# A squared-ReLU MLP: seven block products in place of eight in part of the second product, and a first product in 256 columns

## The chip, the cores and the metric

One core of one Trainium2 chip. The metric is the device time of one execution in microseconds (us), the median of several runs. The engines are named as in the profile: PE is the matrix engine (PEld its loads of the stationary operand), DVE the vector engine, ACT the scalar engine, POOL the general one, SP the queue that issues most DMAs. PSUM is the matrix engine's accumulator memory of eight banks, 512 float32 columns each.

## What is computed

One layer of a decoder: a gated mix of a convolution branch and an attention branch, cross attention, then the MLP, which is where the change lies. SEQ is 256, D_MODEL 1024, D_FF 4096.

```python
        hf = _rmsnorm(h, norm_ffn_g[l]) @ w_ff1[l]
        h = h + jnp.square(jax.nn.relu(hf)) @ w_ff2[l]
    return _rmsnorm(h, norm_final_g)
```

The first product is (256 x 1024)(1024 x 4096), the second (256 x 4096)(4096 x 1024).

## The kernel before

**Split operands.** Every large product is made in float32r with operands split in two: `high` is the operand rounded to float32r (an ACT copy, L189), `low` the rest (a DVE subtraction, issued through `Counted.call`, L77, the line under which all of PE's and DVE's counted work shows). `mm3` (L276) makes one product of three matmuls: high x high, high x low, low x high.

**The weight stream.** All weights come in 1 MB pieces in the order of `STREAM`. `load` (L161) issues the DMA of the next piece on SP into one of three raw buffers, and queues the splitting of its two halves in `high_jobs`; a high queues its low in `low_jobs`; the second low of a piece calls `load` again, so that the next DMA waits until DVE has freed a raw buffer. `weights(kind, i, half, kt)` (L216) hands out a split half; `split_ahead` (L242), called once behind each `weights`, issues one low and one high of later halves. High and low buffers are six each (`HALVES`), counted by `nsplit` and `nused`. If a half is not yet split when it is asked for, `weights` issues splits until it is.

**Order.** Each engine works through its instructions in the order in which the program issues them; the program is one hand-written order. `tick` (L246) steps the generators in `chains`, one `yield` each, so that the work of a later step is issued some matmuls later.

**The first MLP product.** A chunk is 256 of the 4096 hidden columns, as two tiles of 128 (`ct`), each over eight parts of 128 rows of the model dimension (`kt`). Tiles of kind `f1` are "wide" (`is_wide`, L299): per `kt` one matmul of 512 columns (weight high against activation high and low side by side) and one of 256 (weight low against activation high), into both halves of a bank. `activation` (L1082) brings the halves together: ACT evicts one half, DVE adds the other, DVE makes relu(t) times t, ACT makes the high part, DVE the low part.

**The second MLP product.** `ff2` (L1108): for a chunk c, two parts k of 128 hidden columns, two row blocks `rb` of 128 rows and two column halves `hf` of 512, so eight `mm3` of 512 columns a chunk. All 16 chunks accumulate in four banks `dst[rb][hf]`. The loop at L1148 runs the first product two chunks ahead of the second. Behind it the last two chunks (14, 15) are done block by block (`last_products`, L1165), and while PE makes the next block, DVE adds a finished one to the residual (`last_residual`), ACT squares it, and `last_norm` scales and stores a row block.

Of the kernel before, what the change touches and what calls it, by code (L numbers as in the profile page):

```python
# [8 lines left out]
F32 = mybir.dt.float32  # L9
# [3 lines left out]
ALU = mybir.AluOpType  # L13
# [43 lines left out]
HALVES = 6  # L57
EARLY = (3,)
WHOLE = (("conv", 0),)


class Counted:
# [49 lines left out]
def block_kernel(ctx, tc, x, xt, mem, memt, wst, wki, vecs, convw, gout, out):  # L112
# [15 lines left out]
    def t8(name, dt=F32, shape=(P, KT, S)):  # L128
        return big.tile(list(shape), dt, tag="t8", bufs=12, name=name)
# [4 lines left out]
    def w2(name, dt=F32, shape=(P, 512)):  # L134
        return work.tile(list(shape), dt, tag="w2", bufs=8, name=name)
# [25 lines left out]
    def load(parts=1):  # L161
        if nload[0] >= len(STREAM):
            return
        c = nload[0]
        nload[0] += 1
        key = STREAM[c]
        raw = t8(f"raw{c}", F32, (P, N_CHUNK)) if c in EARLY else raws.tile([P, N_CHUNK], F32, tag="raw", name=f"raw{c}")
        n = KT * NK if key[0] == "ki" else N_CHUNK
        src = wki if key[0] == "ki" else wst[INDEX[key]]
        for q in range(parts):  # L170
            ns = slice(q * n // parts, (q + 1) * n // parts)
            nc.sync.dma_start(raw[:, ns], src[:, ns])
        if key in WHOLE:
            whole[key] = raw.rearrange("p (k n) -> p k n", k=2 * KT)
            return
        parts = 1 if key[0] == "ki" else 2
        for q in range(parts):
            ns = slice(q * n // parts, (q + 1) * n // parts)
            high_jobs.append(lambda ns=ns, q=q, last=q == parts - 1: high(key, c, raw, ns, q, last))

    def low_by_dma(key, c, q):

# [2 lines left out]
    def high(key, c, raw, ns, q, last):  # L185
        n = ns.stop - ns.start
        hi = highs.tile([P, N_CHUNK // 2], F32R, tag="hi", name=f"hi{c}_{q}")[:, :n]
        lo = lows.tile([P, N_CHUNK // 2], F32R, tag="lo", name=f"lo{c}_{q}")[:, :n]
        act(hi, raw[:, ns], AF.Copy)  # L189
# [12 lines left out]

        low_jobs.append(low)

    def split_high():
        if high_jobs and nsplit[0] - nused[0] < HALVES - held[0]:
            nsplit[0] += 1
            high_jobs.pop(0)()

    def split_low():  # L210
        if low_jobs:
            low_jobs.pop(0)()

    nsplit, nused, held = [0], [0], [1]

    def weights(kind, i, half, kt):  # L216

        key = (kind, i, half)
        while key not in prepared:
            split_high()  # L220
            split_low()
        nused[0] += 1
        return [w.rearrange("p (k n) -> p k n", k=kt) for w in prepared.pop(key)]


    chains, fill, turn, done = [], [], [0], []
# [852 lines left out]

    start(ff_scale())  # L1080

    def activation(ps, ct, sh, sl):  # L1082
        t = w2(f"ft{ct}", F32, (P, S))
        act(t, ps[:, S:], AF.Copy)  # L1084
        yield
        dve.tensor_tensor(out=t, in0=ps[:, :S], in1=t, op=ALU.add)
        dve.scalar_tensor_tensor(out=t, in0=t, scalar=0.0, in1=t, op0=ALU.max, op1=ALU.mult)
        act(sh, t, AF.Copy)
        yield
        dve.tensor_tensor(out=sl, in0=t, in1=sh.bitcast(F32), op=ALU.subtract)  # L1090

    def ff1(c):
        parts = t8(f"fs{c}", F32R, (P, 4, S))
        jobs = []

        def after(ct, ps):
            jobs.append(start(activation(ps, ct, parts[:, ct % 2, :], parts[:, 2 + ct % 2, :])))

        if c == 0:
            form_b_late("f1", c, f2, after, ps_of=ps_acc)  # L1100
        else:
            form_b("f1", c, f2, after, ps_acc if c == 1 else ps_mm)
        return parts[:, :2, :], parts[:, 2:, :], jobs

    pending = [ff1(0), ff1(1)]
    dst = [[ps_acc(f"ps_ff{rb}{hf}") for hf in range(2)] for rb in range(2)]

    def ff2(c, k, w, x2, rb, hf, cs=slice(0, 512), ps=None, start=False, stop=False):  # L1108
        rows, cols = slice(rb * P, rb * P + P), slice(hf * 512 + cs.start, hf * 512 + cs.stop)
        mm3(dst[rb][hf][:, cs] if ps is None else ps, x2[0][:, k, rows], x2[1][:, k, rows], w[0][:, 0, cols],  # L1110
            w[1][:, 0, cols], start or c == 0 and k == 0, stop)

    hg = turned.rearrange("p (r d) -> p r d", r=2)
    ss = small.tile([P, 2, 3], F32, tag="sso", name="ss_o")
# [5 lines left out]
    def last_residual(rb, ps, lo, hi):  # L1120
        h = h_rm[:, lo // P : hi // P, rb, :]
        ps = by_tiles(ps)
        dve.scalar_tensor_tensor(out=h, in0=ps, scalar=r2[0][:, rb : rb + 1], in1=h, op0=ALU.mult, op1=ALU.add)
# [22 lines left out]
            (nc.scalar if n == 2 else nc.sync).dma_start(out[rb, :, lo:hi], cols)  # L1146

    for c in range(14):  # L1148
        pending.append(ff1(c + 2))
        *x2, jobs = pending.pop(0)  # L1150
        for job in jobs:
            finish(job)
        for k in range(2):
            w = weights("f2", c, k, 1)
            split_ahead()
            for rb in range(2):
                for hf in range(2):
                    ff2(c, k, w, x2, rb, hf)
            tick()
    for *_, jobs in pending:  # L1160
        for job in jobs:
            finish(job)
    ws = {(c, k): weights("f2", c, k, 1) for c in (14, 15) for k in range(2)}

    def last_products(rb, hf, **where):  # L1165
        for (c, k), w in ws.items():
            ff2(c, k, w, pending[c - 14], rb, hf, stop=c == 15 and k == 1, **where)
# [8 lines left out]
    last_products(1, 0)  # L1176
    last_residual(1, dst[1][0], 0, 512)
    last_squares(1, 0, 0, 512)
    last_products(1, 1, cs=slice(0, 256))
    ps = ps_mm("ps_last")[:, :S]  # L1180
    for (c, k), w in ws.items():
        ff2(c, k, w, pending[c - 14], 1, 1, slice(256, 512), ps, c == 14 and k == 0, c == 15 and k == 1)
    last_residual(1, dst[1][1], 512, D)
    last_squares(1, 1, 512, 768)
    last_residual(1, ps, 768, D)
    last_squares(1, 2, 768, D)
    last_norm(1, 2)

# [68 lines left out]
```

## Time and profile before

| what | value |
|---|---|
| median of 3 runs | 508.76 us (508.66 to 508.78) |
| the profiled execution | 508.65 us, span 506.8 us |
| granted PE clock, mean | 0.997 |
| DMA | 100.32 MB, mean 198 GB/s |
| MLP, by the matmuls into `ps_f`, `ps_ff` and `ps_last` | from 322.7 to 500.0 us of the span |

A line of a group reads: line, engine, operation, what it writes and what it reads, shape, count, then busy time in us and mean ns of one, then the engine's idle time just before and who ended most of it. A line of a timeline reads: start in us, duration in us, engine, line, operation, count. Matmuls overlap, and their ends are modelled, so that the distance of their starts is the cost of one in a row. A line of a stretch reads: the stretch, its length, busy time of the engine and its instructions (those that reach in are counted), granted clock, DMA share, GB/s.

### The profile page before, as it was taken

How to read it: one execution, taken by the hardware profiler on the slowest of the kernel's cores; microseconds unless marked ns; L12 is line 12 of the kernel's file. 1: busy time of each engine (PE TensorE's matmuls, PEld its weight loads, DVE VectorE, ACT ScalarE, POOL GpSimd, SP SyncE). 2: the span in 40 equal slices, each digit the busy share in tenths (PEclk: the TensorE clock that was granted, in tenths of full speed). 3: DMA queues.
4: the chain of work that ended last, by engine and by line, in shares of the span. 5: the costliest groups of instructions: out<-in, count | busy, mean ns of one | idle time of the engine just before them, and what ended most of it. 6: DMA issues, size and time to landing. Idle time of an engine off the chain costs nothing.

```text
span 506.8 us, 7855 instructions
## 1 busy us (share of the span) xinstructions
PE 496.5 (98%) x2951; PEld 438.6 (87%) x2951; DVE 419.7 (83%) x806; ACT 314.6 (62%) x565; POOL 31.7 (6%) x49
## 2 busy tenths in 40 slices
PE   7999999999999999999999999999999999999994
PEld 5999998888888888888898999988888888888884
DVE  5999999999999799999899986699755666665565
ACT  7657777878666667678657666575444545544442
POOL 2002212221111100000000000000000000000000
PEclk9999999999999999999999999999999999999998
DMA  8959768899788634437644553445777744455302
GB/s 320 375 185 276 208 182 248 222 262 248 223 279 221 188 113 168 133 116 250 249 164 169 192 214 105 149 157 224 212 242 212 247 167 166 174 211 211 153 1 83
DMA packets 26502, 100.32 MB, mean 198 GB/s; under 512 B 10576, under 2 KB 11472, under 8 KB 15968
## 3 DMA queue, kind: packets, MB, share of 16 engines
q1 hardware_dynamic: 22400, 92.90, 52.5%
q0 software_dynamic: 3632, 6.59, 7.4%
q8 instruction: 23, 0.38, 0.3%
q10 hardware_dynamic: 432, 0.33, 0.2%
q14 instruction: 15, 0.12, 0.1%
HBM read 91.16 MB, written 1.05 MB: 182 GB/s over the span
## 4 chain that ended last, share of the span: by engine, by line
PE 95%; issue 1%; ACT 1%; DMA 1%; DVE 1%; POOLq 0%; POOL 0%; SPq 0%; DVEq 0%; ACTq 0%
PE ps_f L77 18%; PE ps_ff L77 16%; PE ps_conv L77 9%; PE ps_co L77 4%; PE ps_mix L77 4%; PE ps_ao L77 4%; PE ps_q L77 4%; PE ps_k L77 4%; PE ps_ga L77 4%; PE ps_gc L77 4%; PE ps_v L77 4%; PE ps_xo L77 3%; PE ps_qi L77 2%; PE ps_xk L77 2%; PE ps_xv L77 2%; PE ps_xq L77 2%
## 5 line engine op out<-in xcount | busy, mean ns | idle before, releaser
L77 DVE TENSOR_TENSOR lo<-raw,hi 128x1024 fp32r<-128x1024 f32 x163 | 196.8, 1216 | 5.0 <-ACT hi L189 3.4
L189 ACT ACTIVATE hi<-raw 128x1024 fp32r<-128x1024 f32 x163 | 168.8, 1048 | 1.6 <-DMA raw<-in_wst_dram 1.6
L77 PE MATMUL ps_f<-ff_p,hi 128*128 128x512 f32 x256 | 89.5, 396 | 0.0
L77 PE MATMUL ps_ff<-hi,fs 128*128 128x512 f32 (+1 forms) x256 | 80.4, 386 | 0.0
L77 DVE SCALAR_TENSOR_TENSOR acc<-u,cw,acc 128x234 f32<-128x234 f32 (+29 forms) x190 | 78.1, 462 | 0.3
L77 PE MATMUL ps_f<-ff_p,lo 128*128 128x256 f32 x256 | 66.1, 279 | 0.0
L77 PEld LDWEIGHTS ps_ff<-hi,fs 128*128 128x128 f32 x256 | 47.9, 188 | 9.2
L1084 ACT ACTIVATE ft<-ps_f 128x256 f32<-128x256 f32 x32 | 12.3, 383 | 70.0 <-PE ps_f L77 70.0
L77 PEld LDWEIGHTS ps_f<-ff_p,hi 128*128 128x128 f32 x256 | 46.7, 188 | 9.2
L77 DVE TENSOR_TENSOR ft<-ps_f,ft 128x256 f32<-128x256 f32 x32 | 13.5, 422 | 46.0 <-ACT ft L1084 46.0
L77 PEld LDWEIGHTS ps_f<-ff_p,lo 128*128 128x128 f32 x256 | 48.2, 188 | 2.7
L77 PE MATMUL ps_ff<-lo,fs 128*128 128x512 f32 (+1 forms) x128 | 49.4, 386 | 0.0
L77 PE MATMUL ps_conv<-n_p,hi 128*128 128x256 f32 x224 | 41.0, 285 | 0.0
L77 PEld LDWEIGHTS ps_conv<-n_p,hi 128*128 128x128 f32 x224 | 34.9, 192 | 0.8 <-issue 0.7
L77 PE MATMUL ps_conv<-n_p,lo 128*128 128x256 f32 x112 | 31.7, 283 | 0.0
L516 POOL DMA_DIRECT2D acc<-products x25 | 21.6, 866 | 125.3 <-ACT products L515 48.7
L77 PEld LDWEIGHTS ps_ff<-lo,fs 128*128 128x128 f32 x128 | 24.1, 188 | 4.9
L77 PE MATMUL ps_q<-n_p,hi 128*128 128x512 f32 x64 | 23.6, 406 | 0.0
L77 PE MATMUL ps_k<-n_p,hi 128*128 128x512 f32 x64 | 23.5, 407 | 0.0
L77 PE MATMUL ps_ao<-o_p,hi 128*128 128x512 f32 x64 | 22.6, 401 | 0.0
L77 PE MATMUL ps_co<-u_p,hi 128*128 128x512 f32 (+1 forms) x80 | 22.2, 351 | 0.0
L77 PE MATMUL ps_mix<-mix_p,hi 128*128 128x512 f32 (+1 forms) x80 | 22.2, 351 | 0.0
(246 smaller groups left out, 1009.4 us busy)
## 6 DMA issues: line engine op xcount, KB each, us to landing
raw<-in_wst_dram SPq DMA_DIRECT2D x80, 1024.0 KB, 4.9
acc<-products POOLq DMA_DIRECT2D x25, 256.0 KB, 5.0
raw<-in_wst_dram SPq DMA_DIRECT2D x4, 512.0 KB, 7.2
x_rm<-in_x_dram SPq DMA_DIRECT2D x2, 512.0 KB, 4.1
mem_rm<-in_mem_dram SPq DMA_DIRECT2D x1, 1024.0 KB, 8.7
mem_t<-in_memt_dram SPq DMA_DIRECT2D x1, 1024.0 KB, 10.7
h_t<-in_xt_dram SPq DMA_DIRECT2D x1, 1024.0 KB, 7.1
h_rm<-turned SPq DMA_DIRECT2D x16, 64.0 KB, 5.9
```

Of the source, the lines that this page charges most:

```text
L77: return fn(*args, **kwargs)
L189: act(hi, raw[:, ns], AF.Copy)
L516: nc.gpsimd.dma_start(acc[:, ts, :], prod, accum_op=ALU.add)
L1084: act(t, ps[:, S:], AF.Copy)
```

## The change

The chunks fall in three groups: 2, 3, 5, 6, 8, 9, 11 and 12 (`SEVEN`) have their second product made of seven block products; 0, 1, 4, 7 and 10 are made of eight as before, into other banks; 13, 14 and 15 (from `JOINED` on) are done block by block at the end.

- The first product is narrow: per `kt` three matmuls of 256 columns, and both tiles of a chunk share one bank. ACT makes Relu out of PSUM and then Square; nothing is added on DVE.
- For a chunk of seven, four sums of weight blocks are made on DVE (`outer`: two in one operation, `inner`: two, one after the other), four differences of hidden blocks in three DVE operations (`n`), and all of these are split in high and low too. The weights come in four stages: left (2 blocks), last (1), outer (2), inner (2); inner has buffers of its own and takes no slot of the six.
- The halves of `f1` of chunk c + 2 and `f2` of chunk c are split and used alternately: first tile of f1, first half of f2, second tile of f1, second half of f2.
- The seven sums accumulate over all these chunks in seven banks. `combine` adds them to the residual on DVE after the last first-product chunk, and the last three chunks follow.

```diff
+SEVEN = (2, 3, 5, 6, 8, 9, 11, 12)
+JOINED = 13
...
+        if key[0] == "f2" and key[1] < JOINED:
+
+            at = [j.key for j in high_jobs].index(("f1", key[1] + 2, 1))
+            first = len(jobs) // 2
+            high_jobs[at:at] = jobs[:first]
+            jobs = jobs[first:]
+        high_jobs.extend(jobs)
...
+    def seven(key, c, raw):
+
+        b = raw.rearrange("p (k h n) -> p k h n", k=2, h=2)
+        flat = raw.rearrange("p (j n) -> p j n", j=4)
+        t = t8(f"sums{c}", F32, (P, 4, 512))
+        late = t8(f"late{c}", F32R, (P, 2, 2, 512))
+
+        def outer():
+            dve.tensor_tensor(out=t[:, 0:2, :], in0=flat[:, 0:4:3, :], in1=flat[:, 1:2, :].to_broadcast([P, 2, 512]),
+                              op=ALU.add)
+
+        def inner():
+            dve.tensor_tensor(out=t[:, 2, :], in0=t[:, 1, :], in1=flat[:, 0, :], op=ALU.add)
+            dve.tensor_tensor(out=t[:, 3, :], in0=t[:, 2, :], in1=flat[:, 2, :], op=ALU.add)
+
+        def stage(name, src, n, before=None, slot=True):
+            def high():
...
+                act(hi, src, AF.Copy)
+
+                def low():
+                    dve.tensor_tensor(out=lo, in0=src, in1=hi.bitcast(F32), op=ALU.subtract)
+                    prepared[(*key, name)] = (hi, lo)
+                    if name == "inner":
+                        load()
...
+        return [stage("left", b[:, :, 0, :], 2), stage("last", flat[:, 3:4, :], 1),
+                stage("outer", t[:, 0:2, :], 2, outer), stage("inner", t[:, 2:4, :], 2, inner, False)]
...
     def split_low():
         if low_jobs:
             low_jobs.pop(0)()
+        if len(high_jobs) > 1:
+            high_jobs[1].prepare()
...
-        return kind in ("f1", "gc", "ga", "ao", "xk", "q", "k") or (kind in ("mix", "co") and ct < 6)
+        return kind in ("gc", "ga", "ao", "xk", "q", "k") or (kind in ("mix", "co") and ct < 6)
...
+    def activation(c, ct, ps, t, sh, sl):
+        act(t[:, ct, :], ps, AF.Relu)
+        act(t[:, ct, :], t[:, ct, :], AF.Square)
+        yield
...
+        if ct and c < JOINED:
+            n = w2(f"fn{c}", F32, (P, 4, P))
+            if c in SEVEN:
+                dve.tensor_tensor(out=n[:, 0:2, :], in0=flat[:, 1:2, :].to_broadcast([P, 2, P]), in1=flat[:, 0:4:3, :],
+                                  op=ALU.subtract)
+                dve.tensor_tensor(out=n[:, 2, :], in0=flat[:, 0, :], in1=n[:, 1, :], op=ALU.subtract)
+                dve.tensor_tensor(out=n[:, 3, :], in0=flat[:, 2, :], in1=n[:, 2, :], op=ALU.subtract)
...
+        for js, src in cs:
+            act(sh[:, js, :], src, AF.Copy)
+        yield
+        for js, src in cs:
+            dve.tensor_tensor(out=sl[:, js, :], in0=src, in1=sh[:, js, :].bitcast(F32), op=ALU.subtract)
...
+        for name, terms in ((("left", (("1", 0), ("2", 1))), ("last", (("3", 6),))) if half == 0 else
+                            (("outer", (("5", 4), ("7", 3))), ("inner", (("6", 5), ("4", 2))))):
+            w = weights("f2", c, name, None)
+            split_ahead()
+            for j, (bank_name, part) in enumerate(terms):
+                product(bank_name, x.of(part), w, j)
...
     for c in range(14):
+        hidden.append(Hidden(c + 2))
+        ps = ps_mm(f"ps_f{c + 2}")
+        for side in range(2):
+            w = weights("f1", c + 2, side, KT)
             split_ahead()
+            col = ps[:, side * S : side * S + S]
+            tile_b(col, w, f2)
+            hidden[c + 2].after(side, col)
             tick()
+            if c < JOINED:
+                if side == 0:
+                    hidden[c].done()
+                half_of(hidden[c], side)
+                tick()
+    ws = {(c, k): weights("f2", c, k, 1) for c in range(JOINED, 16) for k in range(2)}
...
+    def combine():
+        r, b = r2[0], banks
+        minus = small.tile([P, 2], F32, tag="minus", name="minus")
+        dve.tensor_scalar(minus, r, -1.0, None, ALU.mult)
+        add_to(0, 0, b["2"], r)
+        add_to(0, 1, b["3"], r)
+        add_to(1, 0, b["4"], r)
+        add_to(0, 0, b["1"], r)
+        v, e, g = (w2(f"comb{j}") for j in range(3))
+        act(v, b["1"], AF.Copy)
+        dve.tensor_tensor(out=v, in0=b["6"], in1=v, op=ALU.subtract)
+        dve.tensor_tensor(out=e, in0=b["5"], in1=v, op=ALU.add)
+        add_to(0, 1, e, r)
+        dve.tensor_tensor(out=v, in0=b["7"], in1=v, op=ALU.add)
+        add_to(1, 0, v, minus)
+        dve.tensor_tensor(out=g, in0=b["7"], in1=e, op=ALU.add)
+        add_to(1, 1, g, r)
+
+    for x in hidden[JOINED:]:
+        x.done()
+    combine()
...
+    lasts = [ps_mm("ps_last"), *(banks[name] for name in "2345")]
     for hf in range(2):
-        last_products(0, hf)
-        last_residual(0, dst[0][hf], 512 * hf, 512 * hf + 512)
+        last_products(0, hf, lasts[hf])
+        last_residual(0, lasts[hf], 512 * hf, 512 * hf + 512)
         last_squares(0, hf, 512 * hf, 512 * hf + 512)
     last_norm(0, 1)
```

`add_to` is one DVE operation that scales a block by the row factor and adds it to the residual rows `h_rm`, as `last_residual` does.

More of the change, by code (lines that the diff above doesn't have):

```diff
@@ L175, in load @@
             return
[L176 to L179, printed above, removed]
+        if key[0] == "f2" and key[1] in SEVEN:
+            jobs = seven(key, c, raw)
+        else:
+            parts = 1 if key[0] == "ki" else 2
+            jobs = []
+            for q in range(parts):
+                ns = slice(q * n // parts, (q + 1) * n // parts)
+                jobs.append(Stage((*key, q), lambda ns=ns, q=q, last=q == parts - 1: high(key, c, raw, ns, q, last)))
@@ new lines, in load, with __init__, prepare @@
+        if key[0] == "f2" and key[1] < JOINED:
[4 more added lines that the diff above has]
+        high_jobs.extend(jobs)
+    class Stage:
+        def __init__(self, key, high, before=None, slot=True):
+            self.key, self.high, self.before, self.slot = key, high, before, slot
+        def prepare(self):
+            if self.before:
+                self.before()
+                self.before = None
@@ new lines, in seven @@
+    def seven(key, c, raw):
[11 more added lines that the diff above has]
+            def high():
+                if slot:
+                    hi, lo = ([pool.tile([P, N_CHUNK // 2], F32R, tag=tag, name=f"{tag}{c}{name}")[:, : n * 512]
+                               .rearrange("p (j n) -> p j n", j=n)] for pool, tag in ((highs, "hi"), (lows, "lo")))
+                    hi, lo = hi[0], lo[0]
+                else:
+                    hi, lo = late[:, 0], late[:, 1]
+                act(hi, src, AF.Copy)
[4 more added lines that the diff above has]
+                        load()
+                low_jobs.append(low)
+            return Stage((*key, name), high, before, slot)
+        return [stage("left", b[:, :, 0, :], 2), stage("last", flat[:, 3:4, :], 1),
+                stage("outer", t[:, 0:2, :], 2, outer), stage("inner", t[:, 2:4, :], 2, inner, False)]
@@ L205, in split_high @@
     def split_high():
-        if high_jobs and nsplit[0] - nused[0] < HALVES - held[0]:
-            nsplit[0] += 1
-            high_jobs.pop(0)()
+        if high_jobs and (not high_jobs[0].slot or nsplit[0] - nused[0] < HALVES - held[0]):
+            job = high_jobs.pop(0)
+            nsplit[0] += job.slot
+            job.prepare()
+            job.high()
     def split_low():
@@ L221, in weights @@
             split_low()
-        nused[0] += 1
-        return [w.rearrange("p (k n) -> p k n", k=kt) for w in prepared.pop(key)]
+        nused[0] += half != "inner"
+        return [w if kt is None else w.rearrange("p (k n) -> p k n", k=kt) for w in prepared.pop(key)]
     chains, fill, turn, done = [], [], [0], []
@@ L1092, in ff1 @@
[L1092 to L1111, printed above, removed]
+        flat = t.rearrange("p k (r n) -> p (k r) n", r=2)
+        if c not in SEVEN:
+            cs = [(slice(2 * ct, 2 * ct + 2), flat[:, 2 * ct : 2 * ct + 2, :])]
+        else:
+            cs = [(slice(1, 3), flat[:, 2:4, :]) if ct else (slice(0, 1), flat[:, 0:1, :])]
@@ new lines, in activation @@
+        if ct and c < JOINED:
[5 more added lines that the diff above has]
+                dve.tensor_tensor(out=n[:, 3, :], in0=flat[:, 2, :], in1=n[:, 2, :], op=ALU.subtract)
+                cs.append((slice(3, 7), n))
+            else:
+                dve.tensor_tensor(out=n[:, 0:2, :], in0=flat[:, 0:4:2, :], in1=flat[:, 1:4:2, :], op=ALU.subtract)
+                cs.append((slice(4, 6), n[:, 0:2, :]))
@@ new lines, in activation, with __init__, after, of @@
+        for js, src in cs:
+            act(sh[:, js, :], src, AF.Copy)
+        yield
+        for js, src in cs:
+            dve.tensor_tensor(out=sl[:, js, :], in0=src, in1=sh[:, js, :].bitcast(F32), op=ALU.subtract)
+    class Hidden:
+        def __init__(self, c):
+            self.c, self.jobs = c, []
+            parts = t8(f"fs{c}", F32R, (P, 2, 7, P))
+            self.hi, self.lo = parts[:, 0], parts[:, 1]
+            self.t = w2(f"ft{c}", F32, (P, 2, S))
+        def after(self, ct, ps):
+            self.jobs.append(start(activation(self.c, ct % 2, ps, self.t, self.hi, self.lo)))
+        def of(self, j):
+            return self.hi[:, j, :], self.lo[:, j, :]
+        def row(self, k, rb):
+            return self.of(2 * k + rb)
+        def done(self):
+            for job in self.jobs:
+                finish(job)
@@ new lines, in block_kernel, with product @@
+    hidden = [Hidden(0), Hidden(1)]
+    form_b_late("f1", 0, f2, hidden[0].after, ps_of=ps_acc)
+    form_b("f1", 1, f2, hidden[1].after, ps_acc)
+    uses = {}
+    for c in range(JOINED):
+        for name in ("2", "2", "3", "4", "4", "3", "5", "5") if c not in SEVEN else "1236457":
+            uses[name] = uses.get(name, 0) + 1
+    banks, used = {}, {}
+    def product(name, a, w, j, cs=slice(0, 512)):
+        if name not in banks:
+            banks[name] = {"2": ps_acc, "3": ps_acc, "4": ps_acc, "5": ps_acc, "7": ps_mm}.get(name, ps_aux)(f"ps_p{name}")
+        used[name] = used.get(name, 0) + 1
+        mm3(banks[name], *a, w[0][:, j, cs], w[1][:, j, cs], used[name] == 1, used[name] == uses[name])
@@ new lines, in half_of @@
+    def half_of(x, half):
+        c = x.c
+        if c not in SEVEN:
+            w = weights("f2", c, half, 1)
+            split_ahead()
+            left, right = slice(0, 512), slice(512, D)
+            product("2", x.row(half, 0), w, 0, left)
+            product("4", x.row(half, 1), w, 0, left)
+            product("3", x.of(4 + half), w, 0, right)
+            product("5", x.row(half, 1), w, 0, right)
+            return
+        for name, terms in ((("left", (("1", 0), ("2", 1))), ("last", (("3", 6),))) if half == 0 else
+                            (("outer", (("5", 4), ("7", 3))), ("inner", (("6", 5), ("4", 2))))):
+            w = weights("f2", c, name, None)
+            split_ahead()
+            for j, (bank_name, part) in enumerate(terms):
+                product(bank_name, x.of(part), w, j)
@@ L1159, in block_kernel @@
             tick()
[L1160 to L1165, printed above, removed]
-        for (c, k), w in ws.items():
-            ff2(c, k, w, pending[c - 14], rb, hf, stop=c == 15 and k == 1, **where)
+            if c < JOINED:
[3 more added lines that the diff above has]
+                tick()
@@ new lines, in block_kernel, with last_products, add_to @@
+    ws = {(c, k): weights("f2", c, k, 1) for c in range(JOINED, 16) for k in range(2)}
+    def last_products(rb, hf, ps, cs=slice(0, 512)):
+        cols = slice(hf * 512 + cs.start, hf * 512 + cs.stop)
+        for (c, k), w in ws.items():
+            mm3(ps, *hidden[c].row(k, rb), w[0][:, 0, cols], w[1][:, 0, cols], c == JOINED and k == 0,
+                c == 15 and k == 1)
+    def add_to(rb, hf, ps, scales):
+        h = h_rm[:, 4 * hf : 4 * hf + 4, rb, :]
+        dve.scalar_tensor_tensor(out=h, in0=by_tiles(ps), scalar=scales[:, rb : rb + 1], in1=h, op0=ALU.mult, op1=ALU.add)
@@ L1177, in block_kernel @@
-    last_residual(1, dst[1][0], 0, 512)
+    last_products(1, 0, lasts[2])
+    last_residual(1, lasts[2], 0, 512)
     last_squares(1, 0, 0, 512)
[L1179 to L1183, printed above, removed]
+    last_products(1, 1, lasts[3][:, :S], slice(0, 256))
+    last_products(1, 1, lasts[4][:, :S], slice(256, 512))
@@ L1184, in block_kernel @@
+    last_residual(1, lasts[3][:, :S], 512, 768)
     last_squares(1, 1, 512, 768)
-    last_residual(1, ps, 768, D)
+    last_residual(1, lasts[4][:, :S], 768, D)
     last_squares(1, 2, 768, D)
```

17 lines of the change are left out of this document (removed).

## The prediction

> **What bounds the kernel now.** I read the page's first part, then the chain, then who waited for whom on TensorE.
>
> ```profile
> PE 496.5 (98%) x2951; PEld 438.6 (87%) x2951; DVE 419.7 (83%) x806; ACT 314.6 (62%) x565; POOL 31.7 (6%) x49
> ...
> PE 95%; issue 1%; ACT 1%; DMA 1%; DVE 1%; POOLq 0%; POOL 0%; SPq 0%; DVEq 0%; ACTq 0%
> ...
> PE ps_warm L384 <- DVE zero_r L369: 1.9, 1, 1.9
> PE ps_rsb_n L77 <- POOL rs_n L389: 0.9, 1, 0.9
> PE ps_conv L77 <- DVE n_f L77: 0.6, 1, 0.6
> ```
>
> TensorE is the chain, and the three waits listed are all it ever waited, none of them in the MLP. So a matmul removed there pays in full, but every wait that the change brings is new time. Next, what one MLP chunk costs: stretches of the trace cut at the first matmul of each product, one narrow stage (qi, three tiles), and neighbouring matmuls (start, duration).
>
> ```profile
> core 0: us, PE busy (x), PEclk, DMA share, GB/s
> 33.10:41.74 8.64, 8.64 (x75) 1.00 0.69 238
> 378.51:384.10 5.59, 5.59 (x34) 1.00 1.06 358
> 384.10:389.54 5.44, 5.44 (x26) 1.00 0.27 63
> 477.81:483.39 5.58, 5.58 (x33) 1.00 0.27 112
> ...
> 382.13 0.39 PE L77 MATMUL ps_f<-ff_p,hi 128*128 128x512 f32 x1
> 382.36 0.27 PE L77 MATMUL ps_f<-ff_p,lo 128*128 128x256 f32 x1
> 382.48 0.40 PE L77 MATMUL ps_f<-ff_p,hi 128*128 128x512 f32 x1
> ...
> 62.12 0.28 PE L77 MATMUL ps_conv<-n_p,lo 128*128 128x256 f32 x1
> 62.24 0.40 PE L77 MATMUL ps_conv<-n_p,hi 128*128 128x256 f32 x2
> 62.48 0.28 PE L77 MATMUL ps_conv<-n_p,lo 128*128 128x256 f32 x1
> ```
>
> Durations overlap; starts give the cost. The first product takes 5.59 us a chunk (16 steps of 0.349, one 512 and one 256 wide). The second takes 5.44 (24 matmuls of 0.227). A narrow step, three matmuls of 256, takes 0.360 both in the conv rows and in qi (8.64/24). The granted clock is 1.00 throughout.
>
> **The change, part by part.** The sum is made against the profiled execution: 508.65 us (span 506.8 and 1.85 around it), 0.11 below the median of 508.76.
>
> (1) Eight chunks do 21 matmuls of 512 columns instead of 24: 8 x 3 x 0.227 = **-5.45 us**.
>
> (2) The first product's 256 steps become narrow: 256 x (0.360 - 0.3494) = **+2.7 us**. It has the same columns and one more matmul a step. On the Trainium skill's page "TensorE: Matmul & The Clock Gate", section "Back-to-back issue gap", a matmul costs N/2.4 + 2.5 ns; an estimate by that page is +2.5 ns a step, 0.65 us instead of 2.7. The rows show 10.6 ns, and the rows decide.
>
> (3) DVE and ACT during the MLP. Prices:
>
> ```profile
> L77 DVE TENSOR_TENSOR lo<-raw,hi 128x1024 fp32r<-128x1024 f32 x61 | 73.4, 1221 | 1.8 <-ACT hi L189 0.4
> L189 ACT ACTIVATE hi<-raw 128x1024 fp32r<-128x1024 f32 x61 | 62.5, 1050 | 0.0
> L77 DVE TENSOR_TENSOR ft<-ps_f,ft 128x256 f32<-128x256 f32 x32 | 13.5, 422 | 46.0 <-ACT ft L1084 46.0
> L1088 ACT ACTIVATE fs<-ft 128x256 fp32r<-128x256 f32 x32 | 13.4, 419 | 7.6 <-DVE ft L77 7.5
> L1084 ACT ACTIVATE ft<-ps_f 128x256 f32<-128x256 f32 x32 | 12.3, 383 | 70.0 <-PE ps_f L77 70.0
> L77 DVE TENSOR_TENSOR h_t<-ps_xo,h_t 128x512 f32<-128x512 f32 x3 | 2.1, 692 | 0.7 <-PE ps_xo L77 0.7
> L77 DVE SCALAR_TENSOR_TENSOR h_rm<-ps_ff,ms_ff,h_rm 128x512 f32<-128x512 f32 x4 | 3.0, 748 | 4.2 <-PE ps_ff L77 4.2
> 486.44 2.35 DVE L77 TENSOR_TENSOR lo<-raw,hi 128x1024 fp32r<-128x1024 f32 x2
> ```
>
> Two 1024-wide DVE operations in a row take 2.35, so one behind another costs 1.13; likewise 0.60 for 512, 0.33 for 256 and, off the same slope, 0.20 for 128 (0.29 when it must wait for the one before; bounds 0.16 to 0.42). A seven-product chunk then has on DVE: low parts 5 x 1.13 + 0.60 = 6.25, sums of weights 1.13 + 0.60 + 0.70 = 2.4, differences of the hidden columns (`n`) about 1.0, their low parts 1.1: 10.8 us. TensorE's chunk is 16 x 0.360 + 21 x 0.227 = 10.5. A plain chunk needs about 6 of 11.2. ACT needs near 9 of 10.5 (Relu and Square priced as the 256-wide copies, 0.38 and 0.42). So neither is too slow over three chunks; what counts is the order. What feeds them:
>
> ```profile
> raw<-in_wst_dram SPq DMA_DIRECT2D x27, 1024.0 KB, 4.9
> SPq L172 <- DVE lo L77: 241.3, 47, 10.9
> L189 ACT ACTIVATE hi<-raw 128x1024 fp32r<-128x1024 f32 x163 | 168.8, 1048 | 1.6 <-DMA raw<-in_wst_dram 1.6
> ```
>
> Loads wait for a raw buffer that DVE's last low part frees (241 us of SP waiting), yet ACT waited only 1.6 us for a load: now a freed buffer is next needed two chunks of stream later, some 11 us. The change interleaves halves, so that `f1`'s second low part of one chunk frees the buffer into which the *next* `f2` goes, whose "left" half is split before the next chunk's own `f1` second half. That makes a loop from one such low part to the next: landing 4.9; high of left 1.05; low of left 1.13; `n` 1.0 (issued ahead of what follows, in order); low of last 0.60; outer sum 1.13; low parts of the hidden columns 0.93; low of `f1` 1.22; hand-overs 0.15 = **12.1 us**. Into a plain chunk the parts between fall away: 4.9 + 1.05 + 1.13 + 1.0 + 1.22 + 0.15 = 9.45. From chunk 2 to chunk 12 the loop runs 7 times into a seven-product chunk and 3 times into a plain one: 113 us. TensorE's own way is 7 x 10.5 + 3 x 11.2 = 107.2. Cover at the start: after plain chunk 1 that low part is ready 2.1 us early (Relu and Square 0.9 after the tile, then `n`, last, outer sum, low parts 4.9, against 7.9 until it is used). Left over: 5.8 - 2.1 = **+3.7 us** of waits, on `lo` of `f1`'s second half in the second chunk of a pair. Ends: nothing, if orders that I count as serial overlap, and 6 if loads land later beside the 16 `h_rm` transfers.
>
> (4) `ps_f` now has one bank a chunk with both tiles in it, since product 7 keeps the other. Behind every first tile except that of chunk 15 stand f2 products that hide the Relu. In chunk 15 the second tile follows at once; if it must wait for the Relu, that is the drain 0.16, Relu 0.38 and two hand-overs: **+0.65** (nothing, if columns are kept apart). The Trainium skill's page "PSUM — Partial Sum Buffer", section "PSUM bank collisions raise a hardware error", says that accesses are to be guarded by bank, not by address; no row of before has such a pair, so only the run can show it.
>
> (5) The end. Let E be the moment at which TensorE finishes the first product of chunk 15. Before, that is 483.39 (the row above), and then f2 of chunk 13 covered the last splits. The rows of before's end:
>
> ```profile
> 491.76 0.75 DVE L77 SCALAR_TENSOR_TENSOR h_rm<-ps_ff,ms_ff,h_rm 128x512 f32<-128x512 f32 x1 [2.97 <-PE ps_ff L77]
> 494.48 0.75 DVE L77 SCALAR_TENSOR_TENSOR h_rm<-ps_ff,ms_ff,h_rm 128x512 f32<-128x512 f32 x1 [1.24 <-PE ps_ff L77]
> 495.26 0.69 DVE L77 TENSOR_TENSOR turned<-h_rm,g_out 128x512 f32<-128x512 f32 x1
> 497.48 0.75 DVE L77 SCALAR_TENSOR_TENSOR h_rm<-ps_ff,ms_ff,h_rm 128x512 f32<-128x512 f32 x1
> 498.87 0.74 DVE L77 SCALAR_TENSOR_TENSOR h_rm<-ps_ff,ms_ff,h_rm 128x512 f32<-128x512 f32 x1
> 500.07 0.48 DVE L77 SCALAR_TENSOR_TENSOR h_rm<-ps_last,ms_ff,h_rm 128x256 f32<-128x256 f32 x1
> ```
>
> The last residual started at E + 16.7, just as TensorE ended. Now, behind E, ACT does Relu and Square (0.2 + 0.7), three highs (3 x 0.95) and a copy: E + 4.1. Three halves are still unsplit because the splits keep three pieces ahead (before, the high of f1 15 stands behind the first eviction of f1 14). DVE's last low part ends at E + 5.4, the hidden ones at E + 6.0. Only then, in DVE's order, comes `combine`: seven scaled adds of 0.75, four of 0.69, one tiny, less overlaps: 7.9, to E + 13.9. Then the residuals, spaced as before: 1.42 + 3.0 + 1.39 + 0.93 (the fourth is half as wide now) = 6.7. Last residual at E + 20.6: **+3.9 us**. TensorE alone would be done at E + 17.2, so its own waits there are covered. Ends: 2.5 to 4.5. After this residual nothing changes.
>
> Sum: -5.45 + 2.7 + 3.7 + 0.65 + 3.9 = +5.5; 508.65 + 5.5 = **514.1 us**.
>
> **Rivals.** (a) *No loop*: DVE and ACT keep ahead of TensorE all through. For it: idle of 46 and 70 us in the rows above, and a loop that is only 15% over. Without the 3.7 it is 510.4, with half of it 512.
> (b) *The other side*: the end is hidden. If the last three splits are done before E (splits one or two pieces further ahead than I count), `combine` starts near E + 2, the DVE chain ends at E + 16.6 and TensorE decides: +0.7 in place of +3.9. With no loop, 508.65 - 5.45 + 2.7 + 0.65 + 0.7 = 507.2. It turns at a start of `combine` about E + 2.5; later than this, each us counts. Against it: ACT's three highs cannot precede E in the order of issue.
> (c) *The removed matmuls do not pay*, were a product bound by its weight load. Then 519. Against it: loads of 0.19 us stand under steps of 0.227.
> (d) *The loop is worse*: landings of 7 us instead of 4.9 beside the small transfers in the first pairs, two more us: 516.
>
> **Chances.** Forecast (loop and end, 512 to 515.5): 0.52. (a) 0.23. (b) 0.17, part of it spoilt by waits into no change. (c) and (d) 0.08. About 0.2% (1.0 us) is what a measurement can tell from no change. Faster than 507.7: 0.13, from (b). Within: 0.12, the rest of (b) and the fast side of (a). Slower: 0.75. The range 508.5 to 516 takes in (a) and (d) and leaves out (b) and (c), below 2 in 10.
>
> **What would show it.** 21 product matmuls in such a chunk, 4.76 us, and `ps_f` tiles of 2.88: (1), (2). TensorE waiting near 1 us on DVE `lo` in chunks 3, 6, 9 and 12, and ACT highs waiting for raw DMA: (3). A gap of 0.65 between `ps_f`'s tiles of chunk 15: (4). DVE busy without a break from the last low parts to the last residual, the last residual some 3 us behind TensorE's end: (5). Wrong if TensorE's chain is unbroken through the MLP, or if the last residual again starts as TensorE ends.

## The result, and the profile after

The changed kernel takes **512.64 us** (median of 6 runs, 512.17 to 513.04) against 508.76 for the kernel before (6 runs, 508.66 to 509.02): a ratio of 1.0076, 95% interval 1.0063 to 1.0089. It is slower by 3.9 us; 5.5 had been forecast, and 514.1 us. The profiled execution took 513.04 us with a span of 511.3. The mean granted PE clock is 0.995 (0.997 before); in the stretches of the MLP that are compared here it is 1.00 in both, so this difference is not the clock.

The page of after, in the order in which before was read: engines and the shares of the chain; then who waited for whom on PE.

```profile
PE 497.4 (97%) x3189; PEld 449.5 (88%) x3189; DVE 448.5 (88%) x836; ACT 343.9 (67%) x627; POOL 31.6 (6%) x49
...
PE 84%; DVE 7%; DMA 4%; ACT 2%; issue 2%; POOLq 0%; POOL 0%; DVEq 0%; ACTq 0%
```

```profile
PE ps_last L79 <- DVE fs L79: 1.0, 1, 1.0
...
PE ps_f L79 <- DVE lo L79: 0.7, 1, 0.7
PE ps_f L79 <- ACT ft L1148: 0.5, 1, 0.5
PE ps_last L79 <- ACT ft L1148: 0.5, 1, 0.5
PE ps_last L79 <- DVE lo L79: 0.2, 1, 0.2
```

PE does 238 matmuls more and is busy 0.9 us longer. This total does not say what gave the saving back, since the 0.9 us are already there ahead of the MLP (320.0 us of busy time against 319.1); the stretches below do. The chain was 95% PE and is 84%; DVE and raw loads stand in it now. And PE has five waits in the MLP, where it had none: one on a low part of `f1` (0.7), one on the shared bank (`ft`, 0.5), and three behind the first product (`ps_last`, 1.7 together).

**Up to the end of the first product** little changed. The stretches of PE of the two kernels, from the first matmul of the MLP to E, the end of chunk 15's first product: before, 322.68 to 483.39; after,

```profile
322.86:483.34 160.48, 159.28 (x1062) 1.00 0.56 190
```

So 160.71 became 160.48. The whole gain of 24 matmuls, 5.45 us, shrinks to 0.23 on this way.

**Behind E** it lost 4.5. The timeline of after there, DVE, ACT and PE (start, duration, engine, line, operation; in brackets the idle time before and who ended it):

```profile
484.36 2.94 ACT L250 ACTIVATE hi<-raw 128x1024 fp32r<-128x1024 f32 x3
485.43 3.50 DVE L79 TENSOR_TENSOR lo<-raw,hi 128x1024 fp32r<-128x1024 f32 x3 [2.38 <-ACT hi L250]
488.85 0.75 DVE L79 TENSOR_TENSOR fs<-ft,fs 128x256 fp32r<-128x256 f32 x2
...
489.59 2.72 DVE L79 SCALAR_TENSOR_TENSOR h_rm<-ps_p,ms_ff,h_rm 128x512 f32<-128x512 f32 x4
492.34 0.60 ACT L1299 ACTIVATE comb<-ps_p 128x512 f32<-128x512 f32 x1 [4.74 <-DVE h_rm L79]
492.97 1.42 DVE L79 TENSOR_TENSOR comb<-ps_p,comb 128x512 f32<-128x512 f32 x2 [0.67 <-ACT comb L1299]
...
497.87 0.74 DVE L79 SCALAR_TENSOR_TENSOR h_rm<-ps_last,ms_ff,h_rm 128x512 f32<-128x512 f32 x1
...
502.88 0.28 PE L79 MATMUL ps_p<-hi,fs 128*128 128x256 f32 x1
...
504.49 0.48 DVE L79 SCALAR_TENSOR_TENSOR h_rm<-ps_p,ms_ff,h_rm 128x256 f32<-128x256 f32 x1
```

Three highs still stand behind E, DVE's three low parts follow them, then the hidden low parts, and only then, at 489.59, the first add of `combine`. DVE is busy from there to the last residual, but for two holes. One, of 0.66 at the norm of the first row block, waits for POOL and stood there before the change too. The other, of 0.67, is new: the ACT copy of bank 1 starts when DVE's fourth add, which reads the same bank, is done (ACT had been idle for 4.74), and DVE's next operation needs that copy. The last residual starts at 504.49 (500.07 before, when PE had just ended), 1.6 after PE's last matmul began.

**The loop of raw buffers** is in the chain of after as it had been drawn, but only in places. The chain of waits (start, duration, what), four of its steps:

```profile
393.77 1.15 DVE lo L79
394.93 5.25 DMA raw<-in_wst_dram
400.20 1.07 ACT hi66left L227
...
403.38 1.21 DVE sums L79
404.59 0.67 DVE fs L79 x2
405.26 1.15 DVE lo L79
...
414.58 0.82 DVE lo L79
415.82 5.11 DMA raw<-in_wst_dram
...
422.05 1.22 DVE lo70left L79
...
425.92 1.02 DVE fs L79 x2
426.94 1.15 DVE lo L79
...
437.93 1.15 DVE lo L79
```

From one low part of `f1`'s second half to the next the chain goes: load, high of left, low of left, sums and hidden low parts, low part. The steps take 11.5 us (393.77 to 405.26), 9.3 (to 414.58), 12.4 (to 426.94) and 11.0 (to 437.93); 12.1 and 9.45 had been forecast. (The chain cuts pieces where they overlap; by the starts of the operations on DVE the second and third step are 9.4 and 12.3.) Left and right of this stretch the chain is unbroken PE up to chunk 15.

### The profile page after: what moved, and what is told of

It reads as the page before. It is cut to its first block, busy times and chain, and to the rows that moved or that the text cites. A ratio compares the mean times of both kernels' runs of the same rounds, so it can differ in the third digit from the quotient of the medians.

```text
span 511.3 us, 8405 instructions
## 1 busy us (share of the span) xinstructions
PE 497.4 (97%) x3189; PEld 449.5 (88%) x3189; DVE 448.5 (88%) x836; ACT 343.9 (67%) x627; POOL 31.6 (6%) x49
## 4 chain that ended last, share of the span: by engine, by line
PE 84%; DVE 7%; DMA 4%; ACT 2%; issue 2%; POOLq 0%; POOL 0%; DVEq 0%; ACTq 0%
PE ps_f L79 14%; PE ps_conv L79 9%; PE ps_p L79 9%; PE ps_co L79 4%; PE ps_mix L79 4%; PE ps_ao L79 4%; PE ps_q L79 4%; PE ps_k L79 4%; PE ps_ga L79 4%; PE ps_gc L79 4%; PE ps_v L79 4%; DMA raw<-in_wst_dram 4%; PE ps_xo L79 3%; PE ps_qi L79 2%; PE ps_xk L79 2%; PE ps_xv L79 2%
## 5 line engine op out<-in xcount | busy, mean ns | idle before, releaser
L79 DVE TENSOR_TENSOR lo<-raw,hi 128x1024 fp32r<-128x1024 f32 x147 | 178.0, 1215 | 12.1 <-ACT hi L250 11.7
L250 ACT ACTIVATE hi<-raw 128x1024 fp32r<-128x1024 f32 x147 | 152.7, 1046 | 4.7 <-DMA raw<-in_wst_dram 4.6
L79 PE MATMUL ps_f<-ff_p,hi 128*128 128x256 f32 x512 | 93.4, 283 | 0.5 <-ACT ft L1148 0.5
L79 PEld LDWEIGHTS ps_f<-ff_p,hi 128*128 128x128 f32 x512 | 81.4, 191 | 2.7 <-ACT ft L1148 0.7
L79 PE MATMUL ps_p<-hi,fs 128*128 128x512 f32 (+1 forms) x128 | 38.5, 372 | 0.0
L79 PEld LDWEIGHTS ps_p<-hi,fs 128*128 128x128 f32 x128 | 23.4, 189 | 4.2 <-DVE h_rm L79 0.3
L79 PE MATMUL ps_p<-lo,fs 128*128 128x512 f32 (+1 forms) x64 | 23.7, 371 | 0.0
L79 PE MATMUL ps_ga<-n_p,hi 128*128 128x512 f32 x64 | 22.0, 396 | 0.0
L79 PE MATMUL ps_gc<-n_p,hi 128*128 128x512 f32 x64 | 22.0, 396 | 0.0
L580 ACT ACTIVATE products<-u,cw 128x231 f32<-128x231 f32 (+24 forms) x50 | 21.9, 488 | 0.0
## 6 DMA issues: line engine op xcount, KB each, us to landing
mem_t<-in_memt_dram SPq DMA_DIRECT2D x1, 1024.0 KB, 10.9
```

What stands on the lines that cost most here:

```text
L79: return fn(*args, **kwargs)
L580: act(prod[:, a, s:], u[:, t, : S - s], AF.Copy, scale=cw[:, t, TAPS - 1 - s : TAPS - s])
```

## The experiments

Two batches, the first of four kernels and the second of four, each timed against the kernel before in the same batch (medians 508.79 and 508.81 us, and 508.76 beside the changed kernel). A difference from after is thus one between batches; the kernel before agrees in all of them within 0.05. The theory is that of the prediction: the time is the sum of (1) matmuls saved, (2) narrow first product, (3) loop, (4) shared bank, (5) end. Its rivals are that the slowness is the narrow product alone, or that the loop or the end cost nothing.

### The narrow first product alone

The kernel before, with only the first product's form and its activation changed:

```diff
-        return kind in ("f1", "gc", "ga", "ao", "xk", "q", "k") or (kind in ("mix", "co") and ct < 6)
+        return kind in ("gc", "ga", "ao", "xk", "q", "k") or (kind in ("mix", "co") and ct < 6)
...
-        act(t, ps[:, S:], AF.Copy)
+        act(t, ps, AF.Relu)
+        act(t, t, AF.Square)
         yield
-        dve.tensor_tensor(out=t, in0=ps[:, :S], in1=t, op=ALU.add)
-        dve.scalar_tensor_tensor(out=t, in0=t, scalar=0.0, in1=t, op0=ALU.max, op1=ALU.mult)
```

> The kernel before with the narrow first product alone (three matmuls of 256 columns a step, Relu and Square on ACT, two banks a chunk), eight block products everywhere. Theory: the narrow step costs 0.075 us a tile on TensorE (tiles of 2.87 us in the changed kernel's trace against 2.795), 32 tiles, so +2.4 us on 508.76: 511.2, with no TensorE wait in the MLP. Rival (a matmul costs only its columns, or the freed DVE work shortens something): +0.0 to +0.7, 508.8 to 509.4.

Measured: 511.9 us (511.85 to 512.12), ratio 1.0063 (1.0049 to 1.0076), so +3.1. PE never waited in the MLP. Its stretches of one chunk, cut as for before, first product and second:

```profile
379.75:385.50 5.75, 5.75 (x50) 1.00 1.05 375
385.50:390.97 5.47, 5.47 (x27) 1.00 0.26 41
```

Before it was 5.59 and 5.44. Sixteen times 0.16 is 2.6, close to the forecast's +2.7; the other 0.4 is in the second product, which nothing touched: 5.47 where it was 5.44. There are no waits, and only the first five of its 24 matmuls start more than 0.227 apart (0.228 to 0.236), so this is a cost at the joint between a narrow tile and the 512-wide products. It follows that the narrow form is pure loss for PE in this kernel (DVE, whose busy time falls from 419.7 to 393.6 us, was not the bound), and that term (2) is +3.0 and not +2.7. Whether the changed kernel, in which DVE has more to do and a seventh sum needs a bank, could have kept the wide form, no run shows.

### The load of a seven-product chunk in two halves

The loop goes through the landing of a whole 1 MB piece, though its first stage, left, needs only half of the columns:

```diff
+        if key[0] == "f2" and key[1] in SEVEN:
+            rb, sb = (z.rearrange("p (k h n) -> p k h n", k=2, h=2) for z in (raw, src))
+            for h in range(2):
+                nc.sync.dma_start(rb[:, :, h, :], sb[:, :, h, :])
+            parts = 0
```

> The changed kernel with the raw load of each f2 piece of the seven-product chunks issued as two DMAs of 512 KB, the columns of 'left' first. Theory (the loop over the raw buffer: low part of f1, landing, high of left, ..., next low part): the landing in the loop shrinks by about 2 us, the loop falls under TensorE's 10.5 us, so the three TensorE waits in the MLP (0.2 + 0.9 + 0.3 us) go and the time falls by about 1.4 us to 511.2. Rival (DVE, busy nearly without a break there, is simply too slow for a seven-product chunk): the waits stay, 512.6.

Measured: 511.18 us (511.01 to 512.18), ratio 1.0052 (1.0039 to 1.0065), 1.46 less than after. The longest PE wait on a low part of `f1` is 0.4 in place of 0.7, at the same tile. The expected size came out, but the intervals of the two ratios meet. The traces do not settle it: the second tiles of the first product are late by 0.6 us together here and by 1.4 in after, but by 0.9, 0.5 and 0.5 in three executions below whose loads were not touched. So the loop's cost differs from one execution to the next, between 0.5 and 1.4 us in four traces, and that the halves took it away is supported by the times of this run and not proved. That the loop is real, the next run but one shows.

### First adds of `combine` earlier

The four adds that need nothing but finished banks are issued behind the first tile of chunk 15, instead of behind the last low parts:

```diff
+            if c == JOINED and side == 0:
+                first_adds()
...
-        add_to(0, 0, b["2"], r)
-        add_to(0, 1, b["3"], r)
-        add_to(1, 0, b["4"], r)
-        add_to(0, 0, b["1"], r)
```

> The changed kernel with the first four scaled adds of the combination issued on DVE behind the first tile of chunk 15's first product instead of behind the last splits. Theory (the end is a DVE chain behind TensorE's last first-product tile): these 2.7 us and the 0.65 us wait for ACT's copy of bank 1 leave the chain, the last residual comes some 2 to 3 us earlier until TensorE's own end (about 502.5 in the trace) decides: -1.7 to -2.5 us, 510.1 to 510.9. Rival (the end is bound by TensorE's late start on the last splits): -0.3 at most, 512.3.

Measured: 511.0 us (510.77 to 511.24), ratio 1.0044 (1.0032 to 1.0057), 1.64 less than after. The end of its timeline:

```profile
500.52 0.48 DVE L79 SCALAR_TENSOR_TENSOR h_rm<-ps_p,ms_ff,h_rm 128x256 f32<-128x256 f32 x1 [0.55 <-PE ps_p L79]
502.68 0.48 DVE L79 SCALAR_TENSOR_TENSOR h_rm<-ps_p,ms_ff,h_rm 128x256 f32<-128x256 f32 x1 [1.21 <-PE ps_p L79]
```

DVE now waits for PE at the last two residuals. So DVE's chain was what set the end. 3.4 us were taken off it (four adds, 2.7, and the hole of 0.67); only 1.8 came out at the last residual (504.49 to 502.68), because PE, with its three waits behind E, is late next. And 0.4 of the 1.8 came before E, from a loop that was late by 0.9 in place of 1.4. The time is a tenth above the range expected.

### All of chunks 2 to 12 with seven products

The strongest test of the loop: three chunks more have seven products, so 9 matmuls less, but no plain chunk is left in which the loop could recover.

```diff
-SEVEN = (2, 3, 5, 6, 8, 9, 11, 12)
+SEVEN = (2, 3, 4, 5, 6, 7, 8, 9, 10, 11, 12)
```

> The changed kernel with all of chunks 2 to 12 made of seven products (chunks 4, 7 and 10 too). TensorE does 9 matmuls fewer, -2.0 us by itself. Theory (loop of about 12.1 us a chunk against 10.5 on TensorE): each of ten steps is 1.2 to 1.6 us late, so 10 to 14 us of TensorE waits on lo and some 10 us more in all: 521 to 525. Rival (DVE throughput, 10.8 against 10.5 us a chunk): 3 us of waits, 513 to 514. Rival (waits come from the 16 small transfers beside the first pairs only): 510.6.

Measured: **522.66 us** (522.03 to 523.09), ratio 1.0272 (1.0258 to 1.0286). With less work for PE it is 10.0 us slower than after. PE's waits, a step of the chain of waits, and DVE in this step:

```profile
PE ps_f L79 <- DVE lo L79: 10.0, 8, 1.4
```

```profile
384.42 1.15 DVE lo L79
385.59 5.04 DMA raw<-in_wst_dram
...
391.75 1.23 DVE lo64left L79
392.98 0.35 DVE fn L79
393.34 0.30 DVE fn L79
...
393.67 0.30 DVE fn L79
...
395.62 1.02 DVE fs L79 x2
396.64 1.15 DVE lo L79
```

```profile
384.42:396.64 12.22, 10.95 (x17) 1.00 0.60 194
```

One step is 12.2 us (384.42 to 396.64; forecast for such a step: 12.1) where PE needs 10.5 for the chunk; the eight steps from 371.95 on take 11.9 to 12.5. The loop is real, it is made as described, and in it nothing but a DVE low part is what PE waits for. What sets these steps apart from the 11.5 of after is in three lines: `fn` stands here with three operations, 0.95 us in a row, ahead of the rest. DVE is busy for 10.95 of the 12.22 us and idle once, for 1.2, until ACT has made the high of left from the piece just landed. So the landing adds 1.2 us to a step, and DVE's own work, the rival of this run, is by itself 0.4 longer than PE's 10.5: it is a part of the loss, though not the 10 us.

### One piece more split ahead in chunk 15

```diff
             split_ahead()
+            if c == JOINED:
+                split_ahead()
```

> The changed kernel with one more split_ahead in each half of chunk 15's first product, so that two more highs stand on ACT before the last tile's Relu. Theory (the end is a chain on DVE that starts with the last splits, and the three highs behind the last tile hold it up): the combination starts near 2 us earlier and the last residual with it, 510.4; if ACT then waits for the last raw piece ahead of the Relu of chunk 15's first tile, 1 us of that is lost, 511.4. Rival (the end is bound by the length of the combination and of TensorE's last products alone): no change, 512.6.

Measured: 510.46 us (510.2 to 510.83), ratio 1.0035 (1.0021 to 1.0049), 2.2 less than after. PE's waits for `fs` and `lo` behind E, 1.2 us, are gone from its list; the two on `ft` stay. DVE's first add of `combine` starts at 486.72 instead of 489.59, and the last residual at 501.62 instead of 504.49, both 2.87 earlier. Of this, 0.6 came before E, mostly from a loop that was late by 0.5 in place of 1.4; counted from E, `combine` starts 2.3 earlier, at E + 4.0. So the splits left over behind E are what put `combine` late, and this is the start on which rival (b) of the prediction turns.

### The end rebuilt

All that the runs so far blamed: the first adds and the ACT copy of bank 1 (ahead of the add that reads the same bank) before the first product of chunk 15; one split more ahead; a bank of its own for the second tile of chunk 15; the two sums that need no last split between the splits; and for the first row block, the products of chunks 13 and 14 ahead of those of 15. The last block of products gets a bank of its own too.

```diff
     for c in range(14):
+        if c == JOINED:
+            first_adds()
...
+            if c == JOINED:
+                split_ahead()
+                if side:
+                    col = ps_acc("ps_f15b")[:, :S]
...
+            if c == 15 and k == 1:
+                middle()
...
-    combine()
+    last_adds()
...
-    lasts = [ps_mm("ps_last"), *(banks[name] for name in "2345")]
+    lasts = [ps_mm("ps_last"), *(banks[name] for name in "345"), ps_acc("ps_last2")]
     for hf in range(2):
-        last_products(0, hf, lasts[hf])
+        last_products(0, hf, lasts[hf], chunks=(13, 14))
+    for hf in range(2):
+        last_products(0, hf, lasts[hf], chunks=(15,))
```

> The changed kernel with its end rebuilt and nothing else: first adds of the combination ahead of chunk 15's first product, two sums between the last splits, one more split_ahead a half, a bank of its own for chunk 15's second tile, and the first row block's products of chunks 13 and 14 ahead of those of 15. Theory: the last residual again starts as TensorE ends, and TensorE does not wait behind its last first-product tile; 4.4 us of the end and 0.65 us of the bank wait go, nothing in the MLP's loop: 507.4 to 508.4. Rival (the added 4 us come from somewhere else than the order): 511 or more.

Measured: **507.82 us** (507.65 to 508.44, 11 runs), ratio 0.9981 (0.9973 to 0.9990). PE's timeline: the two tiles of chunk 15, the first matmul behind them, and the last residual.

```profile
476.17 0.40 PE L79 MATMUL ps_f<-ff_p,hi 128*128 128x256 f32 x2
...
479.04 0.40 PE L79 MATMUL ps_f15b<-ff_p,hi 128*128 128x256 f32 x2
...
481.92 0.40 PE L79 MATMUL ps_last<-hi,fs 128*128 128x512 f32 x1
...
499.24 0.48 DVE L79 SCALAR_TENSOR_TENSOR h_rm<-ps_last,ms_ff,h_rm 128x256 f32<-128x256 f32 x1 [0.66 <-PE ps_last L79]
```

The tiles follow each other at 2.87 and 2.88 without a gap (3.51 in after, with the bank shared), `ps_last` starts at once, and the last residual waits for PE again. What PE still waits for in the MLP is 0.3 on a low part of `f1`. This is 4.8 us under the changed kernel. Between the two profiled executions (513.04 and 507.81) it is 5.2, made up of some 3.8 between E and the last residual, 0.6 at the shared bank, and 0.9 in the loop, which no edit touched and which was late by 0.5 here and by 1.4 in after. So 4.5 us are shown to be the order of the end and the shared bank, and without them the change beats the kernel before, barely.

### The end rebuilt, and the halved loads

The two edits above together; no other change.

> e6_end with the f2 loads of the seven-product chunks in two DMAs as in e2_halfload. Theory: both repairs add up, 506.0 to 507.0, faster than the kernel before by 0.4%. Rival (with the end repaired DVE has no room, so the waits come back in another place): 507.4 to 508.4 as e6_end.

Measured: 506.76 us (506.69 to 508.04, 5 runs), ratio 0.9967 (0.9955 to 0.9980): the fastest version, 2.05 under the kernel before. Three of its five runs lie at 506.7; the profiled one took 508.04 and shows PE waiting for the same low parts (1.0 us in two waits). Its second tiles are late by 1.5 us together, as much as in after with whole pieces. The three fast runs lie below all eleven of the kernel without the halves (lowest 507.65), so the halves seem to help in most executions, not in each; but the intervals of the two ratios meet, and no trace at hand is of an execution in which they helped.

### All of seven, with halved loads

Meant to find whether the landing alone makes the loop long:

> e4_all11 with the f2 loads in two DMAs. The loop over the raw buffer (12.2 us in e4_all11's trace) loses about 2 us. If DVE's own work of 10.8 us a chunk then binds against TensorE's 10.5: ten chunks 0.3 to 0.5 us late, 513 to 514. If only the loop mattered: no waits, 509.2. If the split load is worth nothing: 522.7 as before.

Measured: 519.44 us (four runs, 519.36 to 519.48 and one of 526.44), ratio 1.0242 (1.0191 to 1.0294). This is 3.2 less than without the halves and none of the values expected. (The interval is wide because of the one run, which is unexplained, and takes in the ratio without the halves; the 3.2 is that of the other three.) Its chain of waits says why:

```profile
384.43 1.14 DVE lo L79
...
396.49 1.14 DVE lo L79
...
398.30 6.38 DMA raw<-in_wst_dram
404.70 0.63 ACT hi66last L232
...
408.13 1.13 DVE lo L79
...
409.29 4.30 DMA raw<-in_wst_dram
```

The steps are 12.1 (384.43 to 396.49) and 11.6 us, and 11.4 to 12.2 in the five behind them. In six of the eight steps that have a load in the chain it now goes through the *second* half, which `last` waits for: it lands 6.2 to 7.1 us after its issue, later than a whole piece did (5.0). In the other two it goes through the first half, and that lands at 4.3 and 4.9, not at half of 5.0. So the loop was shortened by a few tenths, not by 2 us. It could not have lost 2: DVE is busy for 10.9 to 11.0 us of each of these steps, so that a step without any landing would still be longer than PE's 10.5. No run took the landing out of the loop.

## Why the prediction came out as it did

The forecast was slower with +5.5 us; it is slower with +3.9. The parts and their order were right, one term was more than twice too large, and some luck is in the total: the terms that were too small gave back 0.9 of the 2.3 that this one had too much. Term by term, as in the prediction:

**(1) Removed matmuls, -5.45: right.** The steps of after show 9 and 12 products of 512 columns in 2.07 and 2.75 us (chain of waits), so each removed one is worth its 0.227. Rival (c), products bound by their weight load, is out.

**(2) Narrow first product, +2.7: right in kind, +3.0 in size.** The tiles cost what the rows of `qi` and `ps_conv` had said; the joints with the 512-wide products, not counted, cost 0.4 in all. The lower figure, an estimate of 0.65 from 2.5 ns a matmul by the Trainium skill ("TensorE: Matmul & The Clock Gate", section "Back-to-back issue gap"), does not fit the run with this part alone, +3.1 us; the same section calls its formula that of an isolated matmul and says that a stream of weight loads and matmuls is spaced otherwise.

**(3) Loop of raw buffers, +3.7: the mechanism right, the term too large; 1.4 in the profiled execution.** This is the term that was mis-sized. The late tiles of after are 0.17, 0.94 and 0.30 us over the 2.87 of the others: second tiles of chunks 7, 8 and 11's first product, made in the steps of chunks 5, 6 and 9.

```profile
394.64:397.68 3.04, 3.04 (x25) 1.00 0.49 127
405.37:409.18 3.81, 3.13 (x25) 1.00 0.46 127
438.67:441.84 3.17, 3.12 (x25) 1.00 0.51 150
```

None is late in the steps of chunks 3 and 12. The prediction gave every step into a seven-product chunk the same 12.1 us, with 1.0 for `n` and 0.93 for the low parts of the hidden columns. But the `n` that stands in the loop is that of the chunk whose *first* product was just made, one ahead of the next step's. The timeline of DVE in after:

```profile
381.05 1.22 DVE L79 TENSOR_TENSOR lo<-raw,hi 128x1024 fp32r<-128x1024 f32 x1
...
402.44 0.42 DVE L79 TENSOR_TENSOR fn<-ft 128x256 f32<-128x256 f32 x1
...
423.19 0.42 DVE L79 TENSOR_TENSOR fn<-ft 128x256 f32<-128x256 f32 x1
423.65 0.62 DVE L79 TENSOR_TENSOR fn<-ft,fn 128x128 f32<-128x128 f32 x2
```

In the step from chunk 5 to 6 the hidden chunk is 7, a plain one: one operation of 0.42 and low parts of 0.67 in a row, so 11.5 us. In that from 7 to 8 it is chunk 9, of seven: 1.08 and 1.02, and 12.4 us. So of the seven steps, those from 2 to 3, 5 to 6 and 8 to 9 meet a plain `n`, and from 11 to 12 none; the two of these that lie in the quoted chain take 11.5 and 11.0. With some 11.2 for four steps, 12.1 for three and 9.45 for three, the ten steps are about 109.5 us in place of 113, and behind PE's 107.2 and the cover of 2.1 next to nothing is left.

That more than nothing was measured has a second reason: the prediction weighed the sum of ten steps against PE's sum, but PE waits wherever the loop is behind, and a later plain chunk does not give that time back. Step by step, by the starts of the low parts on DVE and with PE's own 2.87 + 2.75 + 2.87 + 2.07 = 10.56 into a seven-product chunk and 11.24 into a plain one: the step from chunk 4 to 5 takes 12.6 (from 381.05, with a load of 5.5), and the low part, which had been 1.8 ahead, is 0.2 late. That from 5 to 6 takes 11.5, so 0.9 late. Those from 6 to 9 take 9.4, 12.3 and 11.0, together 32.7 for PE's 32.4, so 0.3 late. From 9 on they take 9.3, 11.9 and 10.4 for PE's 32.4, and nothing is late. These are the three late tiles. That the price of a step with `n` of seven was right is shown by the run with all chunks of seven: 11.9 to 12.5 us. The profiled execution is the slowest of the six; in three other traces with the same loop the late tiles come to 0.9, 0.5 and 0.5, so that 1.4 is the upper end of what was seen.

**(4) Shared bank in chunk 15, +0.65: right.** Tile to tile there is 3.51 us for 2.87, and the gap of 0.64 is gone with a bank of its own. The two tiles use different columns of the bank. By the rule of the Trainium skill ("PSUM — Partial Sum Buffer", section "PSUM bank collisions raise a hardware error"), accesses are guarded by bank (more finely, by bank and quadrant of partitions) and not by address, reads like writes; the trace agrees, with PE waiting for ACT's Relu there and 0.64 from it.

**(5) The end, +3.9: right; +4.5.** `combine` started 6.25 behind E (forecast 6.0), and DVE's chain then ran to the last residual at E + 21.15 (forecast 20.6). Of what is missing, 0.25 is this later start, and `combine` itself took 8.3 us up to the first residual for 7.9: the hole of 0.67 before the copy of bank 1 had not been counted, the same rule by bank as in (4), between two readers. The residuals took 6.6 for 6.7. One point was read less well: PE was to be done at E + 17.2, some 3 us ahead of the last residual; its last matmul starts at E + 19.5, 1.6 ahead. Its own waits behind E push it back: the first block of 18 matmuls takes 6.3 us (484.06 to 490.38) where 18 steps of 0.227 are 4.1. This is why taking 3.4 us off DVE's end brought only 1.64.

With the measured sizes: -5.45 + 3.0 + 1.4 + 0.64 + 4.5 = +4.1, against 4.4 between the two profiled executions, from which most of these sizes are taken, and 3.9 between the medians.

**The rivals.** (a), no loop, is refuted by the run with all chunks of seven, though on this kernel the loop is nearer to (a)'s nothing than to the forecast's 3.7. (b), a hidden end, did not come about, since `combine` started at E + 6.25 and not before E + 2.5; but what it says of the end holds, for it gave 507.2 with the end hidden and no loop, and where the splits are further ahead, as it asked, and the end is put in order, the time is 507.82, and 506.76 with halved loads. (d), landings of 7 us in the loop, was not seen: its whole pieces land 4.7 to 5.5 us after issue, the longest of them in the first pairs, beside the small transfers. Pieces issued 1.3 to 2.1 us behind another take 6.2 to 7.7, but none of them stands in the chain.

## What to carry to other kernels

Removing a sixteenth of a product's matmuls is worth only what the surrounding work leaves: here 5.45 us were spent on a narrower form of another product (3.0), on a prefetch that two interleaved streams shortened to one step (1.4) and on a combination put last in the engine's order (4.5), and mending this end turned the loss into a small gain. The loop, whose steps are close to PE's own pace, cost between 0.5 and 1.4 us in four executions, so that one trace did not give its price. Where a new operation needs nothing but data long finished, issue it before the last stretch of dependent work, and check that no other engine reads the same bank just ahead of it. When you price a loop, write the steps out one by one with the chunk that each operation belongs to: an average step hides that work issued in one step belongs to a chunk two further on.

## What the runs showed of the hardware that was not expected

- A matmul in float32r costs 0.227 us at 512 columns and 0.120 at 256 (0.360 for three): worked out from these two widths, 0.42 ns a column and 13 ns that do not depend on the width.
- At a change from a narrow tile to 512-wide products PE loses some 0.03 us (5.47 for 5.44 in the narrow product alone, and 2.75 for 12 x 0.227 = 2.72).
- A 1 MB load as two of 512 KB brings little of it earlier: in the run with all chunks of seven where the chain goes through the first half it lands 4.3 to 4.9 us after its issue, through the second 6.2 to 7.1, and the whole piece took some 5.0. Another 1 MB piece was always issued close behind; no run shows how the halves land without it.
- An ACT read of a PSUM bank was made to wait for a DVE read of the same bank, though both only read: 0.67 us of DVE's time. The rule of the Trainium skill named under (4) asks for a guard between two readers too; no run here shows what would happen without it.
